# A hybrid encoder layer on one core: everything ahead of the gate/up products rewritten as small steps in one fixed order, with f16 projections

## The chip, the cores and the metric

One core of a Trainium2 chip runs the whole program. The metric is the device time of one execution in microseconds (us); several runs are taken and the median is given. Engines are named as in the profile: PE (TensorE, matrix products), PEld (its weight loads), DVE (VectorE), ACT (ScalarE), POOL (GpSimd), SP (SyncE, which issues most DMAs).

## What is computed

Two sequences of 1024 positions, 1024 features each, go through one encoder layer. For the kernel they are 16 tiles of 128 positions (tiles 0 to 7 one sequence, 8 to 15 the other).

```python
h = rms_norm(x, norm1)
proj = h @ w_in                       # 1024 -> 512 q, 128 k, 128 v, 512 gu, 512 gv
a = rms_norm(windowed_gqa(q, k, v, ...), attn_out_gain)   # 8 heads, 2 KV heads, |q-k| <= 128,
                                                          # bias by distance, a sink logit per head
u = gelu(gu); v = rms_norm(gelu(gv), v_gain)
s = einsum("hpq,bcqhd->bcphd", w_s, v) + b_s              # 128x128 mixing inside chunks of 128
g = rms_norm(u * s, gmlp_out_gain)
x = x + concatenate([a, g]) @ w_o
h2 = rms_norm(x, norm2)
x = x + (silu(h2 @ w_gate) * (h2 @ w_up)) @ w_down        # d_ff = 2816
```

Inputs and outputs are float32. Attention of a tile needs the keys and values of the tile before and the tile after, so it can start when the next tile's projection is done.

## The kernel before, in words

All products keep float32 accuracy by splitting each operand into a high and a low half and adding three products (high x high, high x low, low x high). In the input projections the halves are fp32r tiles ("f32" in the profile's forms), made by one ACT copy and one DVE subtraction; probabilities, the output projection, gate/up and down use f16 halves. The output projection, gate/up and down use a seven-product scheme on 2x2 blocks instead of eight block products.

The work has these stages:

1. q products of tiles 0 to 3, k by k, while the weights land (`pq`), then their k/v products (`pkv`), and the bias matrices (`pj`).
2. Attention of tile after tile, with the q and k/v products of tiles 4 to 15 in between. The order comes from a list of events: `at(T + AT[...], fn)` gives each call a time (8 units for a tile), and the list is sorted. Scores are `ps` (L406), with bias and row minimum on DVE (L411), exponentials on ACT (L427), f16 halves of the probabilities (`ph`, L451 and L452), a DMA transposition (`pT`, L459), and products with v (`po`, L472 to L474).
3. The gMLP part. The gv products of the first two tiles (`NFILL = 2`) stand among the last attention steps. After attention a loop over tiles runs the rest of gv (`pgv`) and all of gu (`pgu`), with x loaded and split a second time (L168, L173, L179), the gelu written out as square, multiply, tanh and multiply (L631 to L637), the mixing products for four tiles at a time (`sg`, L652 to L654), and the preparation of the output weights between them.
4. The output projection in eight pairs of tiles (`wa` to `wd`, L843 to L845), the residual, the second norm, and transposition of its result (`ph<-ident,xs`, L927), stored to `t_d` and loaded back as f16 halves (`top`, L970 and L971).
5. Gate/up (`product`, L1052 to L1054), the activation, and the down projection (L1326 to L1328).

The framework's scheduler decides the order on every engine from the order of the calls, dependencies and priorities; only POOL is held to the written order, and only in stage 2. The scheduler also puts waits where a buffer is still in use. SBUF tiles come from tagged pools: `L` 12, `M` 8, `XL` 3, `XN` 3, `S` 9 buffers of 4 KB per partition and 4 large ones (`h16`); PSUM has 4 banks tagged `mm` and 4 tagged `xx`. Nearly all DMAs are issued on SP's queue, in its order.

## Time and profile before

| what | value |
|---|---|
| runs | 1875.27, 1879.43, 1883.58 us; median 1879.43 |
| profiled execution | span 1881.3 us, from the first to the last instruction |
| busy in it | PE 1830.4, PEld 995.6, DVE 1208.1, ACT 1037.0, POOL 112.1 us |
| granted PE clock | 0.990 over the span |
| DMA | 282.06 MB in 216016 packets, mean 150 GB/s |
| first product | at 6.53 us |
| first gate/up product | at 661.41 us |
| first down product | at 1475.46 us |

The profiled execution's span is 1.9 us over the median of the runs. Busy time is not work done: products overlap in the pipe and their ends are modelled, so an engine row near 100% can still hide slow issue. What a product occupies is the distance to the start of the next one.

### The profile page before, as it was taken

The page shows a single profiled execution, that of the slowest core. Times are in us where ns is not written, and L with a number is a line of the kernel's source. Part 1 is how long each engine was busy: PE and PEld are TensorE (multiplying, and loading weights), DVE is VectorE, ACT ScalarE, POOL GpSimd, SP SyncE. Part 2 cuts the span into 40 slices and gives each one's busy share as a digit, 9 for nine tenths or more (in the row PEclk, how much of TensorE's full clock was granted, in tenths as well). Part 3 has the DMA queues.
Part 4 walks back from the last instruction along what each step waited for, and adds up shares of the span by engine and source line. Part 5 has one row for each costly group of instructions (what it writes and reads, how often), then busy time and mean ns, then how long its engine had stood idle before and what let it go on. Part 6 is the DMA issues. An engine that isn't in the chain of part 4 may idle for free.

```text
span 1881.3 us, 26146 instructions
## 1 busy us (share of the span) xinstructions
PE 1830.4 (97%) x9696; PEld 995.6 (53%) x9696; DVE 1208.1 (64%) x2243; ACT 1037.0 (55%) x1946; POOL 112.1 (6%) x143
## 2 busy tenths in 40 slices
PE   8999989999899989999999999999999999999999
PEld 6677757878454444444444444444444444444444
DVE  4887876788876878645645645555556856555661
ACT  6798978776576775534534534444344453333340
POOL 2112100111100000000000000000000000000000
PEclk9999989999999999999999999999999999999999
DMA  7798988333367876313313213223163663333641
GB/s 241 157 191 177 183 159 259 134 135 111 122 232 251 278 244 223 124 40 134 119 61 123 107 73 112 84 96 107 68 227 132 212 219 128 119 101 101 227 142 45
DMA packets 216016, 282.06 MB, mean 150 GB/s; under 512 B 103090, under 2 KB 137906, under 8 KB 215888
## 3 DMA queue, kind: packets, MB, share of 16 engines
q1 hardware_dynamic: 215632, 280.04, 47.9%
q8 instruction: 76, 1.25, 0.3%
q10 hardware_dynamic: 144, 0.26, 0.1%
q14 instruction: 52, 0.43, 0.1%
q0 software_dynamic: 112, 0.09, 0.0%
HBM read 177.04 MB, written 80.23 MB: 137 GB/s over the span
## 4 chain that ended last, share of the span: by engine, by line
PE 58%; DMA 2%; DVE 2%; issue 2%; ACT 1%; POOL 0%; POOLq 0%; SPq 0%; DVEq 0%; ACTq 0%
PE pd L1326 7%; PE pd L1327 7%; PE pd L1328 7%; PE pa L1052 4%; PE pa L1054 4%; PE pa L1053 4%; PE pd L1052 4%; PE pd L1053 4%; PE pd L1054 4%; PE pc L1052 3%; PE pc L1053 3%; PE pc L1054 3%; PE pb L1052 2%; PE pb L1053 2%; PE pb L1054 2%
## 5 line engine op out<-in xcount | busy, mean ns | idle before, releaser
L1326 PE MATMUL pd<-wop,a 128*128 128x512 f16 x616 | 233.5, 379 | 2.3 <-ACT a L109 2.3
L1327 PE MATMUL pd<-wop,a 128*128 128x512 f16 x616 | 233.5, 379 | 0.0
L1328 PE MATMUL pd<-wop,a 128*128 128x512 f16 x616 | 233.3, 379 | 0.0
L1053 PEld LDWEIGHTS <-op 128*128 128x128 f16 x1232 | 120.5, 98 | 149.2 <-issue 7.2
L1052 PEld LDWEIGHTS <-op 128*128 128x128 f16 x1232 | 122.2, 99 | 143.0
L1054 PEld LDWEIGHTS <-op 128*128 128x128 f16 x1232 | 120.5, 98 | 146.2 <-issue 1.1
L1052 PE MATMUL pa<-top,op 128*128 128x512 f16 x352 | 133.4, 379 | 0.7 <-ACT ua L1170 0.7
L1054 PE MATMUL pa<-top,op 128*128 128x512 f16 x352 | 133.4, 379 | 0.0
L1053 PE MATMUL pa<-top,op 128*128 128x512 f16 x352 | 133.4, 379 | 0.0
L109 ACT ACTIVATE wop<-wd,wdr_r 128x512 f16<-128x512 f32 x66 | 47.3, 720 | 152.1 <-PE pd L1328 149.0
L109 ACT ACTIVATE a<-as,asr_r 128x512 f16<-128x512 f32 x154 | 102.1, 709 | 34.3 <-DMA as<-act_d 17.2
L1181 ACT COPY ub<-pc 128x512 f32<-128x512 f32 x44 | 25.7, 584 | 160.3 <-PE pc L1054 160.3
L110 DVE SCALAR_TENSOR_TENSOR a<-as,asr_r,a 128x512 f16<-128x512 f32 x154 | 108.8, 746 | 8.1 <-ACT a L109 6.6
L110 DVE SCALAR_TENSOR_TENSOR wop<-wd,wdr_r,wop 128x512 f16<-128x512 f32 x66 | 49.1, 748 | 99.5 <-ACT wop L109 99.5
L1326 PEld LDWEIGHTS <-a 128*128 128x128 f16 x616 | 60.4, 98 | 75.6 <-ACT a L109 3.3
L1328 PEld LDWEIGHTS <-a 128*128 128x128 f16 x616 | 60.3, 98 | 73.0 <-DVE a L110 0.7
L1327 PEld LDWEIGHTS <-a 128*128 128x128 f16 x616 | 60.3, 98 | 72.2
L995 ACT ACTIVATE junk_e<-g 128x1024 f32<-128x1024 f32 x44 | 46.4, 1054 | 74.4 <-DVE g L1165 74.4
L1187 DVE TENSOR_TENSOR ub<-ub,ua 128x512 f32<-128x512 f32 x44 | 30.4, 691 | 82.0 <-ACT ub L1181 79.6
L427 ACT ACTIVATE sc<-sc,mx 128x384 f32<-128x384 f32 (+1 forms) x128 | 74.6, 584 | 12.9 <-DVE mx L411 12.7
L1162 ACT ACTIVATE g<-g,rs 128x512 f32<-128x512 f32 x57 | 41.1, 722 | 62.5 <-DVE g L1197 35.5
L411 DVE CUSTOM_DVE_ANT_0 sc<-ps,bias 128x384 f32<-128x384 f32 (+1 forms) x128 | 62.3, 519 | 15.3 <-PE ps L406 12.7
(372 smaller groups left out, 4691.8 us busy)
## 6 DMA issues: line engine op xcount, KB each, us to landing
as<-act_d SPq DMA_DIRECT2D x77, 512.0 KB, 3.4
act_d<-g SPq DMA_DIRECT2D x66, 256.0 KB, 2.0
xs<-in_xT_dram SPq DMA_DIRECT2D x28, 512.0 KB, 4.2
tr<-t_d SPq DMA_DIRECT2D x28, 512.0 KB, 5.1
raw<-in_wg_dram SPq DMA_DIRECT2D x24, 512.0 KB, 3.6
raw<-in_wu_dram SPq DMA_DIRECT2D x24, 512.0 KB, 4.7
act_d<-sa SPq DMA_DIRECT2D x44, 256.0 KB, 2.5
act_d<-sb SPq DMA_DIRECT2D x44, 256.0 KB, 2.8
```

What stands on the lines that cost most here:

```text
L109: nc.scalar.mul(hi, src, gain)
L110: nc.vector.scalar_tensor_tensor(lo, src, gain, hi, ALU.mult, ALU.subtract)
L411: nc.vector.tensor_tensor_reduce(out=sc[:, v, :W], in0=ps[v][:, :W], in1=bias[:, h, self.off : self.off + W], scale=1.0, scalar=-NEG, op0= ...
L427: nc.scalar.activation(sc[:, v, :W], sc[:, v, :W], AF.Exp, bias=self.mn[:, h : h + 1], scale=-1.0, accum_out=self.sums[:, h : h + 1],)
L995: nc.scalar.activation(junk_e[0], src, AF.Square, accum_out=acc)
L1052: nc.tensor.matmul(ps, op[:, 0, k, :], th[:, k, :], start=first and k == 0, stop=False, **more)
L1053: nc.tensor.matmul(ps, op[:, 0, k, :], tl[:, k, :], start=False, stop=False, **more)
L1054: nc.tensor.matmul(ps, op[:, 1, k, :], th[:, k, :], start=False, stop=last and k == 3, **more)
L1162: nc.scalar.activation(dst, src, AF.Silu, scale=iv)
L1326: nc.tensor.matmul(ps, a[:, 0, s, cs], wop[:, 0], start=first and n == 0, stop=False, **kw)
L1327: nc.tensor.matmul(ps, a[:, 0, s, cs], wop[:, 1], start=False, stop=False, **kw)
L1328: nc.tensor.matmul(ps, a[:, 1, s, cs], wop[:, 0], start=False, stop=end, **kw)
```

## The change

Everything up to gate/up is cut into steps, each a function with one instruction of one engine, or a few of one engine. The list of steps is sorted by a table, `WHEN`, that has one key for each call, and issued in that order in a region in which every engine keeps the written order. Code outside the region, gate/up and down, stays with the scheduler, which also decides where instructions from outside fall among those of the region. With that:

- x of tiles 4 to 15 is loaded once, multiplied by its row norm (`x_scale`: a product of a diagonal matrix with ones broadcasts the norm along PSUM), split into f16 halves, and stored to `xh_d`; later products load the f16 halves back (`x_back`). Tiles 0 to 3 keep fp32r products for q and k/v and are split into f16 for gv and gu.
- The weights of q, k, v, gv and gu are scaled by a norm of the matrix to fit f16 (`gram`, `scale_*`, `g_sum`) and split into f16 halves; gv's and gu's weights are loaded twice, for the sum and for the split.
- gv products of ten tiles stand among the attention steps, one tile after its q and k/v products; those of tiles 4, 5, 0, 1, 2, 3 (`LATER`) stand near the end of attention. The raw result goes to DRAM (`gv_d`).
- gu and the whole gMLP run tile by tile (`ORDER_G`) before the output projection. Gelu is one ACT instruction (`Gelu_apprx_tanh`) each for gv and gu. The mixing product is 24 products of 64 columns a tile with f16 halves instead of 24 of 256 columns for four tiles.
- The steps of the output projection are the same ones, each with a key; the h2 transpositions of the last pair stand ahead of gate/up. The load of the one-hot matrix, the table and the bias rows moves from POOL's queue to SP's, that of v's gain from ACT's to SP's.

The core of the diff (names of unchanged formulas and most keys left out):

```diff
-AT = dict(
-    loadx=-35.779, xhi=-32.464, xlo=-28.937, rsum=-32.424, rpow=-28.393, proj=-23.482, ...
-)
+LATER = (4, 5, 0, 1, 2, 3)
+ORDER_G = (4, 5, 6, 7, 0, 1, 2, 3, 8, 9, 10, 11, 12, 13, 14, 15)
+WHEN = {
+    "x0_load": [
+        0, 18, 30, 24, 42, 36, 1108, 1278,
+    ],
...
+}
+def plan_order(steps):
+    seen = {}
+    keys = []
+    for n, (fn, _) in enumerate(steps):
+        i = seen[fn.__name__] = seen.get(fn.__name__, -1) + 1
+        keys.append((WHEN[fn.__name__][i] if WHEN else 0, n))
+    return [n for _, n in sorted(keys)]
...
+    def x_diag(t):
+        nc.vector.tensor_scalar(diags[t % 2], ident, rstd1[t], X_NORM, ALU.mult, ALU.mult)
+    def x_row(t):
+        rrow[t] = mm(f"psr{t}", [P, P])
+        nc.tensor.matmul(rrow[t], onec, diags[t % 2], start=True, stop=True)
+    def x_scale(t):
+        nc.vector.tensor_tensor(xst[t], xst[t], rrow[t][:, None, :].to_broadcast([P, KD, P]), ALU.mult)
+    def x_hi(t):
+        hT[t] = k4("S", f"xh{t}", (P, 2, KD, P), F16)
+        nc.scalar.copy(hT[t][:, 0], xst[t])
+    def x_lo(t):
+        nc.vector.tensor_sub(hT[t][:, 1], xst[t], hT[t][:, 0])
+    def x_store(t):
+        store(xh_d[t], hT[t])
+    def x_back(t, z):
+        hT[t, z] = k4("XL", f"xb{t}_{z}", (P, 2, KD, P), F16)
+        load(hT[t, z], xh_d[t])
+    def x16_mm(ps, x, w, ks):
+        for k in ks:
+            xh, xl = x[:, 0, k, :], x[:, 1, k, :]
+            nc.tensor.matmul(ps, xh, w[:, 0, k], start=k == 0, stop=False)
+            nc.tensor.matmul(ps, xh, w[:, 1, k], start=False, stop=False)
+            nc.tensor.matmul(ps, xl, w[:, 0, k], start=False, stop=k == KD - 1)
...
+    def g_sum(z, k):
+        raw = T["graw", z, k // 2, 0][:, k % 2]
+        nc.scalar.activation(raw, raw, AF.Square, scale=g1s[:, k : k + 1], accum_out=gss[:, z, k : k + 1])
...
-        nc.scalar.activation(tt, xg, AF.Square)
-        nc.vector.tensor_scalar(tt, tt, 0.044715 * SQRT_2_PI, SQRT_2_PI, ALU.mult, ALU.add)
-        nc.vector.tensor_mul(tt, tt, xg)
-        nc.scalar.activation(tt, tt, AF.Tanh)
+        nc.scalar.activation(y, y, AF.Gelu_apprx_tanh, scale=cgu[:, 0:1])
...
+    for t in range(GROUP, NT):
+        x_prep(t)
+        for j in range(4):
+            add(q_mm, t, j)
+        for j in range(2):
+            add(kv_mm, t, j)
+        qk_chain(t)
+        if t == 5:
+            g_weights(0)
+        if t not in LATER:
+            gv(t)
+        attention(t - 1)
+    attention(NT - 1)
+    for t in LATER:
+        gv(t)
...
-    with tc.manual_schedule(engines={E.Pool}):
-        for _, _, fn, args in events:
-            fn(*args)
+    with tc.manual_schedule():
+        for n in plan_order(steps):
+            fn, args = steps[n]
+            fn(*args)
```

## Prediction, on record before the change was run

> **What bounds the kernel now.** First the page's span, then the busy time by stage (columns: stretch in us, length, then busy us and instruction count of PE, PEld, DVE, ACT and POOL, the granted PE clock, the share of the DMA engines, GB/s).

> ```profile
> span 1881.3 us, 26146 instructions
> ```
> ```profile
> 0.00:60.00 60.00, 49.68 (x254) 39.03 (x255) 34.20 (x80) 36.41 (x70) 14.19 (x28) 0.97 0.60 195
> 60.00:240.00 180.00, 179.43 (x1733) 136.02 (x1733) 152.11 (x429) 166.11 (x401) 35.09 (x34) 1.00 0.90 188
> 240.00:300.00 60.00, 52.03 (x410) 35.98 (x410) 41.53 (x111) 44.11 (x105) 5.55 (x6) 0.80 0.88 191
> 300.00:472.00 172.00, 166.83 (x774) 138.55 (x773) 130.45 (x255) 128.16 (x226) 21.95 (x31) 1.00 0.43 147
> 472.00:661.00 189.00, 176.82 (x921) 95.33 (x922) 146.01 (x256) 126.27 (x274) 17.84 (x21) 0.98 0.67 220
> 661.00:760.00 99.00, 90.81 (x419) 42.49 (x418) 76.22 (x108) 64.82 (x104) 1.80 (x3) 0.98 0.68 223
> 760.00:1475.00 715.00, 714.67 (x3340) 327.32 (x3339) 399.07 (x667) 320.88 (x537) 14.59 (x21) 1.00 0.30 107
> ```

> PE is the busy engine everywhere, so the question is how much of its time before gate/up is work. From 760 to 1475 us almost nothing but f16 products of 512 columns runs: 715 us / 3340 = 0.214 us each. That is the price of one at full rate. Attention (60 to 240) is nearly balanced: ACT 166 of 180 us, DMA 0.90, and PE never idle. From 240 to 300, where the projections have run out and the last tiles' attention is left, PE idles 8 us and the clock falls to 0.80. The other prices come from the order of PE's instructions in time (start in us, duration, then the instruction; the distance to the next start is what one occupies):

> ```profile
> 6.53 0.79 PE L209 MATMUL pq<-wq_hi,xh_s 128*128 128x512 f32 x1 [6.53 <-ACT wq_hi L105]
> ...
> 10.15 0.39 PE L211 MATMUL pq<-wq_hi,xl_s 128*128 128x512 f32 x1
> ...
> 16.29 0.39 PE L211 MATMUL pq<-wq_hi,xl_s 128*128 128x512 f32 x1
> ...
> 102.73 0.28 PE L210 MATMUL pkv<-wkv,xh 128*128 128x256 f32 x1
> 102.85 0.28 PE L211 MATMUL pkv<-wkv,xl 128*128 128x256 f32 x1
> 103.06 0.44 PE L406 MATMUL ps<-kh,qt 64*128 64x384 f32 x2
> 103.34 0.34 PE L406 MATMUL ps<-kl,qt 64*128 64x384 f32 x2
> 103.52 0.34 PE L406 MATMUL ps<-kh,qt 64*128 64x384 f32 x2
> 103.78 0.20 PE L472 MATMUL po<-v,pT 128*128 128x64 f16 x1
> ...
> 104.29 0.19 PE L474 MATMUL po<-v,pT 128*128 128x64 f16 x1
> 104.32 0.48 PE L209 MATMUL pq<-wq_hi,xh 128*128 128x512 f32 x1
> 104.63 0.40 PE L210 MATMUL pq<-wq_lo,xh 128*128 128x512 f32 x1
> ...
> 111.39 0.27 PE L362 MATMUL pk<-ident,qk 128*128 128x128 f32 x1
> 111.50 0.60 PE L365 MATMUL pt<-ident,qk 128*128 128x128 f32 x4
> ...
> 661.41 0.38 PE L1052 MATMUL pa<-top,op 128*128 128x512 f16 x1
> ```

> Work starts at 6.53 and gate/up at 661.41. The fp32r product of 512 columns: 27 starts from 10.15 to 16.29, 0.227 us. The one of 256 columns: 0.12 from 102.73 to 102.85. A score step (six products): 0.72 from 103.06 to 103.78, and the product before it occupies 0.21 instead of 0.12, so 0.81. A pv product: 17 starts in 0.51, 0.030. A transposition: 0.11. And behind pv an fp32r product occupies 0.31 instead of 0.227, because its weights load longer and a short product doesn't cover that:

> ```profile
> L209 PEld LDWEIGHTS pgv<-wgv_hi,xh 128*128 128x128 f32 x128 | 24.8, 193 | 4.7 <-DVE qt L382 0.2
> ...
> L844 PEld LDWEIGHTS <-mo 128*128 128x128 f16 x224 | 22.1, 99 | 25.3 <-issue 2.2
> ```

> PE's work before gate/up, by these prices: q 384 x 0.227 = 87.2; k/v 384 x 0.120 = 46.1; gv and gu 768 x 0.227 = 174.3; scores 48 steps x 0.81 and 16 of 256 keys at 0.7 (between 0.54 by columns and 0.81) = 50.1; pv 1056 x 0.030 = 31.7; 320 transpositions x 0.11 = 35.2 (16 more come after 661); mixing 96 x 0.120 = 11.5; output projection 672 x 0.214 = 143.8; bias and small ones some 8 (an estimate, the same in both kernels). Sum 587.9 in 654.9 us: **67 us of slack**. About 30 of them are PE's idle time in the first five rows above (10.3 less the 6.5 at the start, 0.6, 8.0, 5.2, 12.2), the rest slow issue: the low clock from 240 to 300, the first products (3.6 us from 6.53 to 10.15 for eight, where 1.8 would do), and the fp32r loads among pv.

> **The change part by part.**

> *Format.* q of 12 tiles 288 x 0.214 = 61.6 and of four in fp32r 21.8; k/v 11.5 for the four, and 288 f16 products of 256 columns that no row shows: between 0.107 (half of the 512-column one) and 0.120, near the former, I take 0.11: 31.7. gv and gu 768 x 0.214 = 164.4. The mixing products become 384 of 64 columns, priced like pv: 11.5. Added: 48 `gram` products of 128 columns, between a transposition (0.11) and a 512-column product (0.23), nearest to the former by columns: 5.3; 16 `x_row`, same ends, 0.17: 2.7. Scores 50.1, pv 31.7, all 336 transpositions 37.0, output projection 143.8 and the 8 stay. Sum 581.1. So f16 saves PE only 7 us of work; the rest must come out of the slack.

> *gv among attention.* A tile's round on PE now is 48 x 0.214 + 24 x 0.11 + 0.55 + 4 x 0.81 + 72 x 0.030 + 0.17 = 19.0 us, where attention now takes 180 / 12 = 15.0 a tile. ACT needs 166.1 / 12 = 13.8 a tile, plus some 0.5 for `gv_out` (half of the 1.06 us for 1024 columns below), so 75% instead of 92%. DMA: 0.90 x 15.0 = 13.5 us a tile, plus 0.79 MB of stores (`xh_d`, `gv_d`), 2.4 us at 220 GB/s / 0.67 = 328 GB/s: 15.9 of 19.0, 84%. SP's queue carries two more issues a tile; a load that waits for its buffer there holds the `pT` transpositions behind it, and pv waits for these:

> ```profile
> PE po L472 <- DMA pT<-ph: 7.8, 8, 2.8
> ```

> The 7.8 us, in eight waits, are what it costs now at DMA 0.90; I expect no more. The DMAs moved off POOL and ACT are four small ones near the start. POOL has 35 of 180 us and the same instructions but for a handful.

> *The end of attention* (8 us idle, clock 0.80 now): six tiles of gv, 6 x 5.1 us of products that depend only on a loaded x, lie ready there, then gu. Most of that slack goes.

> *ACT and DVE.* The written-out gelu and a second split of x go:

> ```profile
> L634 ACT ACTIVATE tt<-tt 128x1024 f32<-128x1024 f32 x16 | 16.9, 1058 | 7.6 <-DVE tt L633 7.6
> ```
> ```profile
> L179 DVE TENSOR_TENSOR xl<-xs,xh 128x1024 fp32r<-128x1024 f32 x28 | 34.2, 1221 | 10.3 <-PE pkv L210 9.0 <-ACT sc L427 1.0 <-ACT xh L173 0.2
> ...
> L633 DVE TENSOR_TENSOR tt<-tt,xg 128x1024 f32<-128x1024 f32 x16 | 19.5, 1222 | 0.3
> ```

> ACT loses the tanh row and the square of the same form ahead of it (some 34), and 12 copies of x as long as that (12); it gains, at half that length each, 16 `gv_out`, 16 weight sums and 16 more weight halves, and three table loads (below), some 30. That is 16 less at most, by halves of a row. DVE loses 19.5, three gelu steps of half that length (29) and 12 subtractions (14.6), and gains 16 `x_scale` of 1.22 (like L633, though one operand is in PSUM) and some 20 for gMLP and weights: some 24 less. Against 501 (ACT) and 504 us (DVE) over the first five stretches, both stay near 78% of the new front. Neither becomes the bound on average; a fixed order that stalls locally is the risk.

> *Output projection* (12.2 idle in 189 now): gMLP, weights and the first pairs' loads now stand ahead of it, so little else competes. *Last pair*: its second norm and transpositions come before gate/up, a chain of a DVE addition and update, an ACT square, POOL's power and an ACT scaling, some 5 us, unless the scheduler sets gate/up products among it as now.

> *Slack that I leave:* start 11 (3.8 and 1.8 as now, and 5 for the norm of the q, k, v weights, which must be complete before their f16 halves are made), attention 8 (0.5 us a tile), its end 4, gu and gMLP 3, output projection 4, last chain 5: **35 us**. Its ends: 12, where only the start and the chain stay; 67, as now. I take the middle: the two largest visible pieces (240 to 300, 472 to 661) lose their cause, the start doesn't.

> *Hand-over.* Gate/up's first ACT copies follow the last `top` conversions on ACT. Now the stretch from 661 to 760 has 8.2 us idle, the hand-over among them; I add 2 us. All that follows stays.

> **Sum.** Gate/up starts at 6.5 + 581.1 + 35 = 622.6. What follows takes 1881.3 - 661.4 = 1219.9, less 1.8 for the transpositions, plus 2: 1842.7. The median lies 1.9 us under this execution's span, so **1841 us**, 2.0% faster. A measurement of this kernel tells a difference from about 0.5% (9 us; the three runs span 8).

> **The rivals.**

> *Nearly no slack* (15 us at the median): 1821. For it: every engine but PE is near 80%, and loads stand far ahead of their use. Against: the start alone has 5.6 now. Chance 0.15.

> *Table loads on the path.* The order puts the last tile's exponentials between gelus of the first gMLP tiles, so ACT's function set changes exp, gelu, exp, gelu, silu: five loads where the trace has two, at

> ```profile
> L97 ACT ACT_TABLE_LOAD x1 | 1.3, 1283 | 0.7 <-PEq L1476 0.7
> ```

> 3 x 1.3 = 3.9 us; if the last tile's chain bound PE there, 1845. gu products that need neither cover it, so 0.10, and the sum takes nothing. [...]

> *Gains given back.* The slack is only moved: PE gets past attention sooner, then waits for gMLP's chain, the output weights (all made in gu's time) and the conversions before gate/up. With 60 to 67 us of slack, 1866 to 1873. For it: ACT and DVE carry as much as before in less time. Against: gu's 16 x 5.1 us cover the preparation. 0.17, of which a third is within 0.5%.

> *Slower.* In a fixed order a DVE or ACT instruction whose input is late holds all behind it, of other tiles too. The place is the 64 score steps, where product, minimum, exponential, halves and transposition pass between four engines through four PSUM banks. Every step that costs PE 0.6 us more eats the 38 us of gain; at 0.75, 1841 + 48 = 1889, slower. For it: ACT is at 92% there now. Against: with gv between them steps are 4.8 us apart instead of 3.8. 0.08, and 0.04 more for between 1870 and 1889.

> The forecast, 1826 to 1860, has the remaining 0.46. **Faster by over 0.5%** (under 1870): 0.15 + 0.10 + 0.46 + 0.11 = 0.82; **within**: 0.06 + 0.04 = 0.10; **slower**: 0.08. The range runs from 1812 (slack 12, and the hand-over's waits gone too) to 1874 (slack 67).

> **What would show it.** Right: gate/up's first product near 620 us; fp32r loads of 193 ns only for tiles 0 to 3, scores and transpositions; no stretch with a clock near 0.80 but the start; ACT near 75% from 60 to 300 us; five table loads. Wrong: PE waits for `pT` or `ps` far over 8 us, or SP held by buffers with PE idle behind it (the slower case); gate/up's start near 600 (the first rival); a start near 622 with gate/up much longer than 814 us (given back). The forecast fails most easily by the size of the slack, above all at the start and in attention.

## The result, and the profile after

The kernel after took **1824.6 us** (median; 1822.2 to 1826.6) against 1881.4 us before (the three runs above and one more), a ratio of **0.970 (95% interval 0.968 to 0.972)**: 3.0% faster, where 2.0% was forecast (1841 us, range 1812 to 1874). The time lies just under the prediction's own band (1826 to 1860) and inside its range. The profiled execution's span is 1822.2 us. Its page's first line, and the busy time by stage (columns as for before):

```profile
span 1822.2 us, 26844 instructions
```
```profile
0.00:60.00 60.00, 51.07 (x278) 42.48 (x279) 38.50 (x89) 42.81 (x82) 11.74 (x23) 0.97 0.67 225
60.00:240.00 180.00, 176.38 (x1585) 112.55 (x1585) 147.84 (x386) 150.30 (x365) 33.12 (x33) 0.99 0.87 211
240.00:300.00 60.00, 60.00 (x552) 36.82 (x553) 50.38 (x131) 53.83 (x126) 8.23 (x8) 1.00 1.03 259
300.00:361.00 61.00, 57.34 (x502) 30.95 (x502) 35.11 (x87) 40.74 (x90) 3.19 (x6) 0.94 0.94 261
361.00:436.00 75.00, 75.00 (x661) 40.80 (x659) 66.02 (x142) 69.76 (x145) 27.00 (x31) 1.00 0.73 245
436.00:606.00 170.00, 169.11 (x890) 90.10 (x889) 139.05 (x232) 126.41 (x270) 12.80 (x19) 1.00 0.83 275
606.00:705.00 99.00, 93.26 (x441) 43.18 (x440) 76.78 (x110) 68.34 (x118) 1.81 (x3) 1.00 0.67 223
705.00:1417.00 712.00, 712.00 (x3329) 326.12 (x3328) 398.25 (x666) 318.97 (x534) 14.59 (x21) 1.00 0.30 108
```

Gate/up starts at 606.6 us, 54.8 earlier than before, and what follows takes 1215.6 us, 4.3 less: nearly the whole gain (54.8 of 59.1 us) lies ahead of gate/up, as forecast. PE is now busy without a break from 240 to 300 us (52.03 of 60 before) and nearly so in the output projection (169.11 of 170). What is left of PE's idle time ahead of gate/up is a short list, in the waits of PE up to 607 us (releaser; us, times, longest):

```profile
PE pq L860 <- ACT wqt L822: 5.5, 1, 5.5
PE pt L1168 <- DVE qk L1159: 2.8, 1, 2.8
PE pgv L955 <- ACT xh L940: 2.8, 1, 2.8
PE ps_s L964 <- ACT gw L1026: 2.6, 1, 2.6
PE pgv L957 <- DVE xh L943: 0.8, 1, 0.8
PE pq L957 <- DVE x_e L919: 0.7, 1, 0.7
PE ps L1202 <- DVE kl L1181: 0.6, 1, 0.6
PE wa L1601 <- ACT sc L1609: 0.6, 1, 0.6
```

Two more waits take 0.3 and 0.2 us. The 7.8 us that PE waited for `pT` before are gone. Three of the waits are followed by a stretch at a low granted clock (0.79, 0.66, 0.72):

```profile
54.00:62.00 8.00, 5.85 (x28) 4.03 (x28) 7.23 (x17) 6.30 (x14) 3.87 (x2) 0.79 0.61 198
...
74.00:79.00 5.00, 4.51 (x26) 3.80 (x27) 4.56 (x21) 4.40 (x14) 2.48 (x2) 0.66 0.95 190
...
306.00:318.00 12.00, 8.40 (x47) 3.82 (x44) 7.53 (x17) 10.26 (x22) 0.55 (x1) 0.72 0.96 309
```

So the slack can be accounted for. By the prediction's own prices it is 606.6 - 5.5 - 581.1 = **20 us**, not 35: some 11 us of waits (all but the first row, which lies ahead of the first product), 6.7 us of slow clock (0.21 x 8 + 0.34 x 5 + 0.28 x 12), and some 2 us for the first products (5.52 to 9.91 us, where their prices give 2.3). It is what is left beside the priced work, so it is as good as those prices: after's timeline has an f16 product of 512 columns at 0.2155 us (eleven starts from 302.80 to 305.17) instead of 0.214, 2.6 us over 1728 of them, and an `x_row` at 0.30 instead of 0.17, 2 us over 16.

### The profile page after: what moved, and what is told of

It is laid out like the page before. It is cut to its first block, busy times and chain, and to the rows that moved or that the text cites. A ratio compares the mean times of both kernels' runs of the same rounds, so it can differ in the third digit from the quotient of the medians.

```text
span 1822.2 us, 26844 instructions
## 1 busy us (share of the span) xinstructions
PE 1793.5 (98%) x10070; PEld 903.5 (50%) x10070; DVE 1179.4 (65%) x2181; ACT 1021.3 (56%) x1955; POOL 113.6 (6%) x141
## 4 chain that ended last, share of the span: by engine, by line
PE 90%; DVE 4%; DMA 3%; ACT 2%; issue 2%; POOL 0%; POOLq 0%; SPq 0%; DVEq 0%; ACTq 0%
PE pd L2318 7%; PE pd L2320 7%; PE pd L2319 7%; PE pd L1824 4%; PE pa L1824 4%; PE pd L1825 4%; PE pa L1825 4%; PE pa L1826 4%; PE pd L1826 4%; PE pc L1824 4%; PE pc L1825 4%; PE pc L1826 4%; PE ps L1202 2%; PE pb L1824 2%; PE pb L1825 2%; PE pb L1826 2%
```

## The experiments

Stages of every run are read from its profiled execution in the same way: when gu's last product starts (gu ends), how long the output projection takes from its first product to its last, and when gate/up starts. The time is the median; before took 1881.1 to 1881.4 us beside every group of runs.

| kernel | time, us | ratio to before (95%) | gu ends | output projection | gate/up starts |
|---|---|---|---|---|---|
| before | 1881.4 | | 471.4 | 188.5 | 661.4 |
| after | 1824.6 | 0.968 to 0.972 | 434.8 | 170.3 | 606.6 |
| order on POOL alone | 1892.6 | 1.004 to 1.007 | 486.7 | 183.8 | 672.1 |
| order on PE, POOL | 1889.2 | 1.003 to 1.007 | 489.5 | 179.5 | 670.5 |
| order on DVE, POOL | 1871.0 | 0.993 to 0.996 | 467.0 | 186.4 | 655.0 |
| order on ACT, POOL | 1850.1 | 0.982 to 0.985 | 455.4 | 173.8 | 630.7 |
| order on ACT, DVE, POOL | 1825.2 | 0.969 to 0.974 | 434.9 | 170.6 | 607.0 |
| gv behind attention | 1874.8 | 0.994 to 0.998 | 475.6 | 170.9 | 648.1 |
| the same, PE and SP free | 1871.5 | 0.994 to 0.997 | 482.2 | 170.6 | 654.4 |
| before, f16 halves | 1868.6 | 0.991 to 0.996 | 455.9 | 189.4 | 647.8 |
| before, fixed order | 2034.4 | 1.080 to 1.084 | 622.6 | 189.3 | 813.4 |
| no gelu tables | 1824.2 | 0.967 to 0.971 | 434.3 | 170.3 | 606.1 |
| one more ACT copy a step | 1832.7 | 0.973 to 0.977 | 440.8 | 171.6 | 613.9 |
| two places mended | 1825.5 | 0.969 to 0.972 | 435.4 | 170.6 | 607.6 |

The theory at the start was the prediction's: the slack goes because of what now stands where (gv among attention, little beside the output projection). The rivals were the fixed order as such, and the f16 format.

**Order kept on POOL alone.** The same steps in the same sequence, but the scheduler orders PE, ACT, DVE and SP:

```diff
-    with tc.manual_schedule():
+    E = mybir.EngineType
+    with tc.manual_schedule(engines={E.Pool}):
```

> The kernel after, with the written order kept on POOL alone; PE, ACT, DVE and SP are ordered by the scheduler from the same emission order. Theory (the gain comes from what stands among attention and from what no longer stands in the output projection): the content of each stage is the same, so 1825 to 1835 us. Rival 'order' (the fixed order on every engine is itself the gain): the slack comes back, gate/up starts near 650 and the time is 1860 to 1875. Rival 'format' (the f16 weight loads are most of it): under 1835.

1892.6 us. The theory fell: with the same steps in the same written sequence, but the engines' order left to the scheduler, the kernel is 68 us slower than after and 0.5% slower than before. gv still runs among attention (its products start from 107.7 to 361.1 us, in after from 104.2 to 331.2). From 60 to 420 us all engines do less; this run's row, then the same of after:

```profile
60.00:420.00 360.00, 325.54 (x2811) 195.91 (x2811) 246.96 (x638) 272.79 (x636) 51.11 (x56) 0.96 0.84 209
```
```profile
60.00:420.00 360.00, 352.71 (x3133) 211.80 (x3132) 283.34 (x711) 301.68 (x699) 68.01 (x72) 0.99 0.89 234
```

No engine is at its bound: they wait for each other. The waits of ACT, DVE and PE in that stretch, in this run and then in after:

```profile
ACT sc L1229 <- DVE mx L1213: 39.8, 24, 6.0
...
DVE ph L1254 <- ACT ph L1249: 35.8, 28, 8.6
...
PE ps L1202 <- DVE mx L1213: 8.1, 8, 2.0
PE pgv L955 <- ACT gr L1312: 5.7, 1, 5.7
```
```profile
ACT sc L1229 <- DVE mx L1213: 17.4, 19, 4.9
...
DVE ph L1254 <- ACT ph L1249: 4.3, 7, 1.8
```

DVE waits 35.8 us instead of 4.3 for ACT's half of a probability tile, and PE waits for ACT's copies of gv. What ACT does first is read here at one place, PE's longest such wait, on ACT's own timeline of this run (start, duration, instruction, and in brackets what it waited for), then on PE's:

```profile
318.93 0.72 ACT L1298 ACTIVATE o<-o,a_r 128x512 f32<-128x512 f32 x1 [0.75 <-POOL a_r L1295]
321.28 1.15 ACT L1408 ACTIVATE wss<-wss,cst 128x1024 f32<-128x1024 f32 x1 [1.63 <-DMA wss<-in_w_o_dram]
...
322.54 1.15 ACT L1408 ACTIVATE wss<-wss,cst 128x1024 f32<-128x1024 f32 x1
...
323.69 0.56 ACT L1312 COPY gr<-pgv 128x512 f32<-128x512 f32 x1
```
```profile
316.52 0.38 PE L957 MATMUL pgv<-wg,xh 128*128 128x512 f16 x1
...
324.31 0.58 PE L955 MATMUL pgv<-wg,xb 128*128 128x512 f16 x1 [5.71 <-ACT gr L1312]
```

A gv product set was complete at about 317 us and only had to be copied out of its bank. ACT stood 1.63 us waiting for the load of an output weight, squared it and the next one, whose sum PE first reads at 419.2 us (`ps_w`, L1412), and copied gv at 323.69. PE, out of banks, idled 5.71 us.

**Which engine's order it is.** The same line, with other engines named:

```diff
-    with tc.manual_schedule():
+    E = mybir.EngineType
+    with tc.manual_schedule(engines={E.Pool, E.Activation, E.DVE}):
```

In the other three runs the set is POOL and PE, POOL and ACT, or POOL and DVE.

> The kernel after with the written order kept on ACT, DVE and POOL, while PE and SP are ordered by the scheduler. With POOL's alone it took 1892.6 us, and PE then waited most for ACT's copies of gv and for DVE's score minima. Theory 'the engines that serve PE' (PE loses its time because ACT and DVE do other work ahead of what it waits for): most of the 68 us return, 1825 to 1845. Rival 'PE's own order' (the scheduler spreads products and score steps badly): 1870 to 1895. In between if both.

> The mirror image: the written order kept on PE and POOL, while ACT, DVE and SP are ordered by the scheduler. Theory 'the engines that serve PE': 1865 to 1895, since PE in a fixed order waits just as long for a late copy. Rival 'PE's own order': 1825 to 1845.

> The kernel after with the written order kept on ACT and POOL; PE, DVE and SP are ordered by the scheduler. With POOL's alone PE waited 18 us for ACT's late copies and 8 us for DVE's minima before 420 us, DVE's subtractions waited 36 us for ACT's halves, and ACT's exponentials 40 us for DVE's minima. Theory 'ACT' (its order is the one that counts, DVE follows what ACT hands it): 1825 to 1840. Rival 'both needed': 1850 to 1880. Rival 'DVE': 1880 or more.

> The mirror image: the written order kept on DVE and POOL; PE, ACT and SP are ordered by the scheduler. Theory 'ACT': 1875 to 1895, as with POOL's order alone. Rival 'both needed': 1850 to 1880. Rival 'DVE': 1825 to 1840.

ACT's and DVE's order together give 1825.2 us, all of after's gain; PE's order gives 1889.2, 3.4 of the 68 us, with an interval that overlaps that of POOL alone. So it is "the engines that serve PE", and PE's and SP's order can be left to the scheduler. Of the 67.4 us, ACT's order alone returns 42.5 (1850.1) and DVE's alone 21.6 (1871.0), nearly a sum (64.1): both are needed, ACT's counts twice as much. In the output projection it is mostly ACT's: 173.8 us with its order fixed, 186.4 with DVE's, 183.8 with POOL's alone.

**gv behind attention.** The order stays fixed on every engine; the keys of ten tiles' gv steps are moved, and all that stands behind them by as much:

```diff
+AT_GV, GV_LEN = 31780, 520
+for _n, _v in WHEN.items():
+    for _i, _k in enumerate(_v):
+        if (_k >= AT_GV or _n == "gm_load") and _n not in ("gv_mm", "gv_out", "gv_store"):
+            _v[_i] = _k + 10 * GV_LEN
...
+for _n in range(10):
+    for _j in range(4):
+        WHEN["gv_mm"][4 * _n + _j] = AT_GV + GV_LEN * _n + 130 * _j
...
+            add(x_again, t)
```

The key 31780 lies behind tile 13's attention, the ten tiles are 6 to 15, and `x_again` loads a tile's halves from `xh_d` once more.

> The kernel after, its order still fixed on every engine, with the gv products of tiles 6 to 15 taken out of attention and put in one block behind tile 13's attention, each from an x loaded again (0.5 MB a tile). Theory: a round of attention falls from 19.2 us only to what ACT needs, 15.5 us busy less 0.6 for the gv copy, at 95% some 15.7 us, while 5.2 us a tile come back behind: 10 x (15.7 + 5.2 - 19.2) = 17 us slower than after, 1835 to 1850. Rival 'order' and rival 'format': order and format are as in after, so within 5 us of it, 1820 to 1830.

1874.8 us, slower than the theory gave. The runs spread from 1866.8 to 1877.7 us, and the profiled one, with a span of 1864.7 us, is the fastest. The 51.8 us of gv products (240 x 0.216) taken out of attention shorten it little: in that execution gate/up starts 41.5 us later than in after, so some 42 of the 52 us had been free there (50 by the medians). The expectation's step that failed is that ACT would then set the round. This run's rows:

```profile
60.00:240.00 180.00, 153.75 (x1469) 104.01 (x1469) 150.21 (x393) 149.29 (x363) 34.80 (x33) 0.93 0.88 205
240.00:300.00 60.00, 54.16 (x469) 32.40 (x469) 51.58 (x136) 53.60 (x127) 6.60 (x7) 0.97 1.07 271
```

ACT is busy 149.29 of 180 us, as in after (150.30), and PE idles 26 us and runs at 0.93. So neither is full. The likely reading is that each tile's chain sets the round (DVE's norm of q and k, minimum, exponential, transposition) in the engines' given order, and that gv's products are what PE does meanwhile; it is argued, not shown, since PE's waits from 60 to 300 us are spread over that chain, the longest sums being 6.3 us for `pT` and 4.3 for the minima. To see whether PE's own fixed order was to blame, the same kernel with PE and SP free:

> The run with the gv products of ten tiles behind attention (1874.8 us), now with PE and SP ordered by the scheduler and the written order kept on ACT, DVE and POOL. Theory (gv among attention is itself worth its time: without it PE has nothing to do while a tile's chain of norm, exponential and transposition passes, whatever PE's order): 1862 to 1880. Rival (it was PE's fixed order, written for rounds with gv, that held it): 1830 to 1850.

1871.5 us: it was not. The 5.2 MB of x loaded again are in the price too, and what they cost wasn't measured apart. What these two runs can't tell is what ACT's and DVE's order would give if it were planned anew for a kernel without gv among attention; it is still the one spaced for gv. That was not tried, so the 42 us (50 by the medians) are an upper end for gv's place by itself.

**A fixed order on the kernel before.** Its attention part is a list of timed events; the same change of one line there, the other way round:

```diff
-    with tc.manual_schedule(engines={E.Pool}):
+    with tc.manual_schedule():
```

> The kernel before with the order of its attention part (its list of timed events) fixed on every engine instead of POOL alone; nothing else. Theory (a fixed order pays only with work written for it): 1870 to 1890, within 10 us of before. Rival (a fixed order pays by itself): 20 us or more faster, under 1861.

2034.4 us, 8% slower, far outside what either side expected. PE's largest waits from 60 to 420 us:

```profile
PE ps L406 <- DVE kl L379: 55.5, 11, 7.1
PE pk L362 <- DVE qk L357: 27.2, 13, 7.1
```

Taken literally, the list of events sets the score steps behind DVE steps that come too late, eleven times in these 360 us. An order is no gain by itself: it has to be made for its steps and their latencies.

**The format alone, in the kernel before.**

```diff
-        hi = k4("S", f"xh{t}", (P, KD, P), F32R)
+        hi = k4("S", f"xh{t}", (P, KD, P), F16)
...
```

The low half of x and the halves of the weights change in the same way.

> The kernel before with the halves of x and of the q, k, v, gv and gu weights in f16 instead of fp32r, nothing else; the scaling of x and of the weights by their norms that the kernel after adds is left out. Theory: products get 0.011 us cheaper, 384 x 0.011 for q, 384 x 0.011 for k/v, 768 x 0.011 for gv and gu = 17 us of PE's work, of which the half in attention is not bound by PE: 1861 to 1873 us. Rival 'format': 40 us or more of the 57 us of gain, 1830 to 1841. Rival 'order': as the theory.

1868.6 us, 12.5 us faster than before in the same group of runs, as the theory had it and far from the rival's 40. The way back, fp32r in the kernel after, was not tried: two fp32r halves don't fit x's one buffer.

**The table loads.**

```diff
-        nc.scalar.activation(y, y, AF.Gelu_apprx_tanh, scale=cgu[:, 0:1])
+        nc.scalar.activation(y, y, AF.Tanh, scale=cgu[:, 0:1])
...
```

The same for gu. This kernel leaves the gelu out, so what it computes is no longer the layer; it serves for the time alone.

> The kernel after with Tanh in place of the gelu function, which leaves the gelu out and with it the three extra table loads at 341.1, 359.5 and 364.4 us (1.283 us each). Theory: PE waits for nothing there, so within 2 us of after, 1822 to 1827. [...]

1824.2 us: with 1952 ACT instructions instead of after's 1955, three table loads fewer, nothing changes. They were as the prediction had them, five in after: the two that before has too, and these three:

```profile
L1323 ACT ACT_TABLE_LOAD x2 | 2.6, 1283 | 0.0
...
L1229 ACT ACT_TABLE_LOAD x1 | 1.3, 1283 | 0.0
```

**More work for ACT.**

```diff
+        nc.scalar.copy(ph[:, 0, 0], T["sc", t, hp][:, 0, :W])
         nc.scalar.copy(ph[:, 0], T["sc", t, hp][:, :, :W])
```

> The kernel after with one more ACT copy of 128x384 at each of the 64 score steps, 0.40 us each by the 0.51 and 0.74 us that 512 and 768 columns occupy: 1.6 us of ACT a tile, 26 us in all. Theory (ACT has room in a round of 19.2 us, of which it is busy 15.5): 1825 to 1831. Rival (ACT still sets the round): 1845 to 1852.

1832.7 us, 8 us slower than after: between the two. Of some 26 us of added ACT work about a third arrives. ACT goes from 150.30 to 160.99 busy us of 180, and PE from 176.38 to 173.14:

```profile
60.00:240.00 180.00, 173.14 (x1535) 109.44 (x1534) 141.96 (x374) 160.99 (x391) 32.52 (x32) 0.98 0.86 204
```

ACT is not the bound, but its room isn't free either. A likely reason is that every copy also lengthens the chain that it stands in; no run shows that apart.

**Two of the remaining waits mended.**

```diff
+WHEN["x_hi"][14], WHEN["x_lo"][14] = 28430, 28560
+for _f, _k in (("scale_mm", 7240), ("scale_add", 7245), ("scale_pow", 7250)):
+    WHEN[_f][1] = _k
```

The keys of tile 2's halves were 29256 and 29421, those of the column sums 7060, 7114 and 7283.

> The kernel after with two places of its order changed: the f16 halves of tile 2's x are made 7 us earlier (PE waits 2.8 and 0.8 us for the halves at 309 us and then runs 6 us at half the clock, 6.6 us in all), and the column sums of gv's weights go behind two more score steps (a wait of 2.6 us at 74.5 us). Theory (each wait costs what it shows, and the next in line is ready): 7 to 10 us faster than after, 1814 to 1818. Rival (what follows was waiting as well, so the waits only move): 1822 to 1826.

1825.5 us, no gain: the rival. Both waits are gone, and at both places the score steps next in line now wait for DVE's minima. At the second, after's PE timeline and then this run's:

```profile
309.57 0.39 PE L955 MATMUL pgv<-wg,xh 128*128 128x512 f16 x1 [2.76 <-ACT xh L940]
...
311.02 0.61 PE L957 MATMUL pgv<-wg,xh 128*128 128x512 f16 x1 [0.84 <-DVE xh L943]
```
```profile
306.40 0.38 PE L962 MATMUL pgv<-wg,xh 128*128 128x512 f16 x1
308.28 0.92 PE L1207 MATMUL ps<-kh,qt 64*128 64x384 f32 x2 [1.50 <-DVE mx L1218]
...
310.84 0.68 PE L1207 MATMUL ps<-kh,qt 64*128 64x384 f32 x1 [1.17 <-DVE mx L1218]
```

In both kernels the stall at this second place starts further back, with an engine that waits for a transposition DMA: ACT in after, DVE in this run:

```profile
306.19 0.83 ACT L1249 CAST ph<-sc 128x768 f16<-128x768 f32 x1 [4.25 <-DMA pT<-ph]
```
```profile
307.66 0.56 DVE L1218 CUSTOM_DVE_ANT_0 sc<-ps,bias 128x384 f32<-128x384 f32 x1 [3.68 <-DMA pT<-ph]
```

Scores, halves and half of the transposed tiles share one pool of eight buffers (`M`), so a late transposition holds the next tile that needs a buffer there; ACT's halves of x stood behind that wait in its order. The new keys take them out of that place, but the late transposition is still there. The DMA share there is 0.96 in after (306 to 318 us); why the transposition came late was not tried. No run that computes the layer was faster than the kernel after.

## Why the prediction was right, and where it was not

*The sum.* Gate/up was put at 622.6 us and came at 606.6: 1.0 us from the start (5.5 for 6.5) and 15.0 from the slack, 20 for 35: the slack is the term that was mis-sized. The tail was put at 1220.1 us and took 1215.6: in its first 99 us PE idles 5.7 us instead of 8.2 and the clock is 1.00 instead of 0.98. Together that is the 20.5 us between 1842.7 and 1822.2. The work, 581.1 us, is short by the two prices above, some 5 us at most; the others that after's rows show agree (0.109 for an f16 k/v product, 0.030 for pv, 0.82 for a score step). The low end of the range rests on a slack of 12 us for the start and the last chain, but the prediction's own terms for these, 11 and 5, make 16.

*The slack, term by term.* The start came out right as a total: 11 us forecast; its waits (2.8, 2.6, 0.7, 0.6), the slow clock behind them (3.4) and the first products (2) make 12. But 5 of the 11 were for the norm of the q, k, v weights, and PE waits for no such thing; it waits for the first tile's q and k chain and for the column sums of gv's weights instead. That the totals agree is luck. Attention got 8 and took almost none: from 79 us on PE hardly idles until 306. Its end got 4 and took 7, all at the one place at 306 to 318. gu and gMLP (3) took none, the output projection (4) one. The last chain (5) took none, because the scheduler laid gate/up's first products among the last pair's transpositions; the prediction had named that exception. The sign "no stretch with a clock near 0.80 but the start" fails at that one place (0.72). So the rival "nearly no slack" (15 us, 1821) is nearer than the forecast's own figure; by this one measurement its 0.15 looks too little.

*The reason for the slack* is the step that failed. The prediction said that the two largest pieces lose their cause because of what stands there: products that lie ready at the end of attention, and little beside the output projection. With the same steps and the scheduler's order, gu ends at 486.7 us, later than before (471.4), and the output projection takes 183.8 us, 4.7 less than before instead of 18.2. What takes the slack out of the new steps is the written order of ACT and DVE (67 of the 68 us), which the prediction treated as a risk alone ("a fixed order that stalls locally"). It did name the mechanism, an ACT or DVE instruction that holds those behind it, but on the wrong side: at the place that was read, the scheduler's order has it and the written one hasn't (in after no wait of PE ahead of gate/up is for a copy of gv). That the time came inside the range although the order had no term in the sum is luck. What stands where is not without worth: given the order, gv behind attention costs up to some 42 us, while the output projection keeps its 170.9 us. So the gain needs both, and the prediction had one. Whether before's own 67 us of slack came from its order is not shown: the one fixed order that was tried there made it slower.

*gv among attention.* A round on PE was put at 19.0 us. It holds: q starts 147.6 us apart over eight tiles (115.9 to 263.5), 18.5 us. That PE would set it holds too. ACT was put at 75% from 60 to 300 and was at 85% (204.1 of 240), DMA at 84% a round and was at 0.87 from 60 to 240.

*Format.* The prediction had 16.6 us less of q, k/v, gv and gu products, and 7 net of what the change adds. The 12.5 us of f16 by itself in the kernel before, where nothing is added, fit the 16.6. The fp32r loads stay where they were said to stay, and with the added `gram` and `x_row` products.

```profile
L955 PEld LDWEIGHTS <-xh 128*128 128x128 f16 x304 | 30.0, 99 | 25.8 <-issue 4.1 <-ACT xh L940 3.1
...
L1202 PEld LDWEIGHTS ps<-kh,qt 64*128 64x128 f32 x256 | 25.5, 190 | 9.6 <-issue 5.0 <-DVE misc L929 0.8 <-DVE mx L1213 0.8
```

*The rivals.* "Table loads on the path" is refuted: a load takes 1283 ns in after, 3.8 us for the three, and without them the time is the same within 0.4 us, less than the runs spread. "Gains given back" did not occur: gate/up to the end is 4.3 us shorter, where 2 us more had been added for the hand-over. "Slower" is real as a mechanism at one place (306 us), where ACT stood 4.25 us for a transposition and tile 2's halves of x stood behind it, and the fixed order on the kernel before shows its size where the order doesn't fit: 153 us.

## What to carry to other kernels

When PE is the bound and other engines serve it, look at the order of the serving engines first: preparation that is needed late, put ahead of a copy that empties a bank, can cost PE its duration and the wait for its load besides (at the place shown, 4.0 us of ACT, from 319.65 to 323.69). Moving work is worth what the order makes of it: here the same steps gained 3.0% with ACT and DVE in a written order and lost 0.5% without, and a written order that wasn't made for its steps lost 8%. Before you mend a wait, read what the next instructions in that queue wait for, and follow the named engine back to its own wait: two mended waits of 6.2 us together brought nothing.

## What the hardware showed beside this

In after's profile the granted clock is 1.00 or 0.50 in all one-microsecond windows ahead of gate/up but these:

```profile
54.00:55.00 1.00, 0.10 (x1) 0.10 (x2) 1.00 (x3) 0.97 (x3) 0.00 (x0) 0.61 0.07 8
...
57.00:58.00 1.00, 1.00 (x4) 0.62 (x3) 0.48 (x2) 0.88 (x3) 1.00 (x1) 0.68 0.44 74
...
74.00:75.00 1.00, 0.51 (x4) 0.49 (x4) 0.96 (x3) 0.93 (x4) 0.00 (x0) 0.85 1.04 192
...
78.00:79.00 1.00, 1.00 (x10) 0.72 (x8) 0.93 (x6) 0.97 (x4) 0.00 (x0) 0.94 0.97 295
...
310.00:311.00 1.00, 0.18 (x1) 0.00 (x0) 1.00 (x2) 0.70 (x3) 0.00 (x0) 0.61 0.13 51
...
317.00:318.00 1.00, 1.00 (x6) 0.46 (x5) 0.35 (x2) 1.00 (x3) 0.03 (x1) 0.98 1.40 361
```

In the run with two places mended PE's pauses at the second place were shorter, 1.50 us (until 308.28) and 1.17 (until 310.84), yet the clock fell: products of one form start 0.21 us apart ahead of them (305.97 to 306.40) and 0.40 behind them (312.10 to 312.50), and the mean granted clock from 240 to 315 us is 0.96. So in these two runs the length of a pause alone didn't decide whether the clock fell. Most of PE's work between and behind the two pauses was score steps; whether that matters was not tested.
